# Uneven stores for two octets, work on the last loads moved behind older work, and the last Q evacuation on two engines, in a one-core linear ReLU attention kernel

## The chip, the cores and the metric

One core of a Trainium2 chip. The metric is the device time of one execution in microseconds (us). The span in a profile runs from the first to the last instruction of one profiled execution and is some 1.8 us shorter than that time. A core has five compute engines (PE does matmuls, DVE and ACT elementwise work, POOL, but for building the identity matrix, and SP here only issue transfers) and sixteen DMA engines that move all data between HBM and the on-chip memory.

## The reference

```python
batch, heads, seq, dim = 8, 12, 512, 64           # float32
Q_feat, K_feat = np.maximum(0, Q), np.maximum(0, K)
KV    = np.einsum('bhkd,bhkv->bhdv', K_feat, V)    # 64 x 64 per head
K_sum = np.sum(K_feat, axis=2)
numerator   = np.einsum('bhqd,bhdv->bhqv', Q_feat, KV)
denominator = np.einsum('bhqd,bhd->bhq', Q_feat, K_sum)
return numerator / (denominator[:, :, :, None] + 1e-10)
```

Three inputs of 12.58 MB are read and one output of the same size is written: 50.33 MB for very little arithmetic.

## The kernel before

The 96 heads are handled in 12 octets of 8 heads. Each octet has two groups g of K and V (256 KB each on chip, as bf16) and one Q. `prep` makes the masked bf16 operands, `mm_kv` forms K^T V and the sum of K, `transp` and `evac_qt` transpose Q and apply the ReLU, `mm_out` and `norm` (three rounds) give the output, `store` writes 1 MB. Order on each engine is the order of the program. The cut below is shortened, and its comments are added.

```python
def evac_qt(o, i):
    ...
    for z in range(2):
        nc.scalar.activation(qtz[o % NZ][:, z, us, :, z, :], pv[:, :, :, z, :], Act.Relu)

def store(o, o_sb):
    if o + DELAY < NO:       # a dummy copy: holds the store until K of octet o+5 has landed
        nc.sync.dma_start(out=scratch, in_=k_sb[2 * (o + DELAY)][0:1, 0, :])
    parts = 2 if o == NO - 1 else 1
    ...                      # whole store of 128 rows of 8 KB; the last octet's in two halves
# ...
for o in range(NO + 1):      # octet o is prepared while octet o-1 is put out
    if o < NO:  mm_kv(2 * o); evac_kv(2 * o)
    if o > 0:   mm_out(o - 1, 0); norm(o - 1, 0, o_sb)
    if ahead:   prep(2 * o + 2); prep_act(2 * o + 2)
    if o > 0:   mm_out(o - 1, 1); norm(o - 1, 1, o_sb)
    if o < NO:  mm_kv(2 * o + 1); evac_kv(2 * o + 1); ...   # and Q of octet o
    if ahead:   prep(2 * o + 3); prep_act(2 * o + 3)
    if o > 0:   mm_out(o - 1, 2); norm(o - 1, 2, o_sb); store(o - 1, o_sb)
```

All loads but the first four are issued from POOL and cast from float32 to bf16 on the way (one software queue); all stores are issued from SP (one hardware queue). Both queues run on the same sixteen DMA engines (point 2 of the prediction; here the two account for 73.9% and 27.1% of the sixteen engines' time).

## Time and profile before

| | before |
|---|---|
| time, median of 6 runs | 128.02 us (127.97 to 128.18) |
| profiled span | 126.2 us |
| HBM traffic | 50.33 MB, 399 GB/s over the span |
| last two half stores issued | 119.02 us and 1 us later |
| last mark of the last store | 125.28 us |

A *mark* is the moment at which one DMA engine reports that its share of one transfer has landed; a transfer over sixteen engines leaves sixteen marks in the trace. They are read here from the trace's record of semaphore updates, sorted by time; the record does not say which engine a mark comes from. The page and the stages of this kernel are shown in the prediction. One more view carries the argument, the waits of SP's queue (waiting line, what it waited for: us in total, times, longest):

```profile
SPq L197 <- DMA k_sb<-in_K_dram: 71.9, 7, 41.3
SPq L197 <- DMA scratch<-k_sb: 22.8, 6, 4.3
SPq L202 <- DVE o_sb L187: 9.0, 4, 5.9
```

SP's time goes into waiting for K, on purpose: stores are held back so that loads run first, and a backlog of finished octets is left for the end. Little of its waiting is for results (9.0 us in this row).

### The profile page before, as it was taken

How to read it: one execution, taken by the hardware profiler on the slowest of the kernel's cores; microseconds unless marked ns; L12 is line 12 of the kernel's file. 1: busy time of each engine (PE TensorE's matmuls, PEld its weight loads, DVE VectorE, ACT ScalarE, POOL GpSimd, SP SyncE). 2: the span in 40 equal slices, each digit the busy share in tenths (PEclk: the TensorE clock that was granted, in tenths of full speed). 3: DMA queues.
4: the chain of work that ended last, by engine and by line, in shares of the span. 5: the costliest groups of instructions: out<-in, count | busy, mean ns of one | idle time of the engine just before them, and what ended most of it. 6: DMA issues, size and time to landing. Idle time of an engine off the chain costs nothing.

```text
span 126.2 us, 4865 instructions
## 1 busy us (share of the span) xinstructions
PE 77.3 (61%) x2112; PEld 68.3 (54%) x2112; DVE 80.6 (64%) x210; ACT 76.9 (61%) x169; POOL 32.1 (25%) x62
## 2 busy tenths in 40 slices
PE   0032917978397956534997647389964793797200
PEld 0041907967386845434986646178953692696100
DVE  3256785698936959673669787528828628774900
ACT  0165891599198798660799949508917925958000
POOL 6902424325243331241143133033113000000000
PEclk9999999999859999996799999955999679769995
DMA  3999999999999999999999999999999999999992
GB/s 106 374 309 213 214 208 209 217 206 218 205 215 209 208 214 324 257 216 325 256 215 301 280 214 281 301 212 214 347 235 216 316 266 216 352 418 410 416 384 104
DMA packets 10757, 32.81 MB, mean 260 GB/s; under 512 B 1392, under 2 KB 1392, under 8 KB 9328
## 3 DMA queue, kind: packets, MB, share of 16 engines
q0 software_dynamic: 8064, 17.83, 73.9%
q1 hardware_dynamic: 2384, 13.63, 27.1%
q10 hardware_dynamic: 288, 1.05, 2.1%
q8 instruction: 16, 0.26, 0.7%
q14 instruction: 5, 0.04, 0.1%
HBM read 37.75 MB, written 12.58 MB: 399 GB/s over the span
## 4 chain that ended last, share of the span: by engine, by line
DMA 32%; PE 27%; issue 13%; ACT 11%; DVE 10%; ACTq 1%; SPq 0%
DMA v_sb<-in_V_dram 25%; PE ps_out L174 13%; PE ps_kv L139 11%; DMA kv_first<-in_K_dram 7%; ACT kvd L146 5%; ACT qt L159 4%; PE ps_qt L153 3%; DVE o_sb L187 3%; DVE qt L121 3%; ACT vo L134 3%; DVE kf L128 2%; DVE vo L130 1%; DVE rec L186 1%; ACTq L267 0%; DVE kvd L118 0%
## 5 line engine op out<-in xcount | busy, mean ns | idle before, releaser
L139 PE MATMUL ps_kv<-vo,kf 128*128 128x130 bf16 x384 | 32.5, 248 | 21.9 <-ACT vo L134 11.7
L174 PE MATMUL ps_out<-kvd,qt 128*32 128x130 bf16 x1536 | 33.7, 243 | 16.7 <-issue 13.3
L139 PEld LDWEIGHTS <-kf 128*128 128x128 bf16 x384 | 27.8, 112 | 25.3 <-DVE vo L130 16.3
L174 PEld LDWEIGHTS <-qt 128*32 128x32 bf16 x1536 | 27.0, 107 | 21.9 <-issue 15.3
L146 ACT CAST kvd<-ps_kv 64x130 bf16<-64x130 f32 x96 | 25.2, 263 | 16.7 <-PE ps_kv L139 14.8
L134 ACT ACTIVATE vo<-v_sb,mask 128x1024 bf16<-128x1024 bf16 x22 | 26.2, 1190 | 13.9 <-DMA v_sb<-in_V_dram 13.8
L187 DVE TENSOR_TENSOR o_sb<-ps_out,rec 128x768 f32<-128x768 f32 (+1 forms) x36 | 31.3, 868 | 1.4
L159 ACT ACTIVATE qt<-ps_qt 128x512 bf16<-128x512 bf16 x48 | 24.8, 603 | 0.3
L128 DVE TENSOR_SCALAR kf<-k_sb,mask 128x1024 bf16<-128x1024 bf16 x44 | 19.1, 476 | 8.6 <-DMA k_sb<-in_K_dram 8.6
L85 POOL DMA_DIRECT2D k_sb<-in_K_dram x22 | 12.8, 583 | 39.1 <-DMA q_sb<-in_Q_dram 24.1
L184 DVE TENSOR_SCALAR den<-ps_out 128x12 f32<-128x12 f32 (+1 forms) x36 | 5.9, 164 | 17.9 <-PE ps_out L174 17.8
L153 PE MATMUL ps_qt<-ident,q_sb 128*128 128x128 bf16 x192 | 15.7, 245 | 2.4 <-issue 2.4
L87 POOL DMA_DIRECT2D v_sb<-in_V_dram x22 | 12.3, 557 | 17.1 <-DMA k_sb<-in_K_dram 7.3
L153 PEld LDWEIGHTS <-q_sb 128*128 128x128 bf16 x192 | 14.0, 112 | 2.6 <-issue 2.5
L130 DVE TENSOR_SCALAR vo<-v_sb,mask 128x1024 bf16<-128x1024 bf16 x22 | 10.6, 481 | 2.1 <-DMA v_sb<-in_V_dram 2.1
L186 DVE RECIPROCAL rec<-den 128x12 f32<-128x12 f32 (+1 forms) x36 | 7.9, 220 | 1.2
L91 POOL DMA_DIRECT2D q_sb<-in_Q_dram x12 | 6.5, 542 | 7.8 <-DMA v_sb<-in_V_dram 4.1
L128 DVE TENSOR_SCALAR kf<-kv_first,mask 128x1024 bf16<-128x1024 f32 x4 | 2.8, 750 | 4.9 <-DMA kv_first<-in_K_dram 4.9
L134 ACT ACT_TABLE_LOAD x1 | 1.3, 1283 | 5.8 <-DMA kv_first<-in_V_dram 5.8
L121 DVE MEMSET qt<- 128x2048 f32 x2 | 3.5, 1765 | 0.8 <-issue 0.8
L134 ACT ACTIVATE vo<-kv_first,mask 128x1024 bf16<-128x1024 f32 x2 | 2.4, 1180 | 2.6 <-DMA kv_first<-in_V_dram 2.6
L130 DVE TENSOR_SCALAR vo<-kv_first,mask 128x1024 bf16<-128x1024 f32 x2 | 1.5, 747 | 0.0
(12 smaller groups left out, 3.5 us busy)
## 6 DMA issues: line engine op xcount, KB each, us to landing
out_dram<-o_sb SPq DMA_DIRECT2D x11, 1024.0 KB, 9.2
q_sb<-in_Q_dram POOLq DMA_DIRECT2D x12, 512.0 KB, 14.9
k_sb<-in_K_dram POOLq DMA_DIRECT2D x22, 256.0 KB, 13.8
v_sb<-in_V_dram POOLq DMA_DIRECT2D x22, 256.0 KB, 13.2
kv_first<-in_V_dram ACTq DMA_DIRECT2D x2, 512.0 KB, 7.3
kv_first<-in_K_dram SPq DMA_DIRECT2D x2, 512.0 KB, 7.0
out_dram<-o_sb SPq DMA_DIRECT2D x2, 512.0 KB, 5.1
scratch<-k_sb SPq DMA_DIRECT2D x7, 0.1 KB, 5.1
```

The costliest lines, as they stand in the source:

```text
L85: nc.gpsimd.dma_start(out=k_sb[g].rearrange("p r d -> p (r d)"), in_=Kr[g])
L87: nc.gpsimd.dma_start(out=v_sb[g].rearrange("p r d -> p (r d)"), in_=Vr[g])
L128: nc.vector.tensor_scalar(kf[g][:, :, s, :], k_sb[g], scalar1=0.0, scalar2=mask[:, 0, s:s + 1], op0=Alu.max, op1=Alu.mult)
L130: nc.vector.tensor_scalar(vo[g % NB][:, :, 0, 0:D], v_sb[g], scalar1=mask[:, 1, 0:1], scalar2=None, op0=Alu.mult)
L134: nc.scalar.activation(vo[g % NB][:, :, 1, 0:D], v_sb[g], Act.Copy, scale=mask[:, 1, 1:2])
L139: nc.tensor.matmul(ps_kv[g], kf[g][:, r, :, :].rearrange("p s d -> p (s d)"), vo[g % NB][:, r, :, :], start=(r == 0), stop=(r == R - 1), s ...
L146: nc.scalar.copy(kvd[g % NK][64 * c:64 * c + 64, :, s, c, :], ps_kv[g][64 * s:64 * s + 64])
L153: nc.tensor.transpose(ps_qt[o, i][:, u, :], q_sb[o][:, i * (U // 2) + u, :], ident)
L159: nc.scalar.activation(qtz[o % NZ][:, z, us, :, z, :], pv[:, :, :, z, :], Act.Relu)
L174: nc.tensor.matmul(po[hs, b, c:c + 2 * D1], qtf[o % NZ][:, z, u * P + 32 * w:u * P + 32 * w + 32], kvd[(2 * o + h // 4) % NK][:, h % 4 // ...
L186: nc.vector.reciprocal(rec, den)
L187: nc.vector.tensor_tensor(o_sb[:, 2 * u0:2 * (u0 + nu)].rearrange("p (b r) d -> p b r d", b=2), pv[:, :, :, 0:D], rec.unsqueeze(3).to_broa ...
```

## The change

Intent: give engines that have less to do more rows of a store; keep the in-order engines from standing at loads that come late in the last two octets; halve the last evacuation of Q by using two engines.

```diff
-    def evac_qt(o, i):
+    def evac_qt(o, i, eng=None):
...
         for z in range(2):
-            nc.scalar.activation(...)
+            if eng is nc.vector:
+                eng.tensor_scalar(qtz[o % NZ][:, z, us, :, z, :], pv[:, :, :, z, :], scalar1=0.0,
+                                  scalar2=None, op0=Alu.max)
+            else:
+                nc.scalar.activation(...)
...
+    def cuts(o):
+        return ((16, P), (0, 5), (5, 10), (10, 15), (15, 16)) if o in (1, 3) else ((0, P),)
...
+        for p0, p1 in cuts(o):
+            nc.sync.dma_start(out=Ov[p0:p1], in_=o_sb[p0:p1])
...
     for o in range(NO + 1):
...
+        if o < NO - 1:
+            kv(2 * o)
+        if o > 0:
+            out_round(o - 1, 0, o_sb)
+        if o < NO - 2:
+            prepare(2 * o + 2)
+        if o > 0:
+            out_round(o - 1, 1, o_sb)
+        if o < NO - 1:
+            kv(2 * o + 1)
+            qt(o)
+        if o < NO - 2:
+            prepare(2 * o + 3)
+        if o > 0:
+            out_round(o - 1, 2, o_sb)
             store(o - 1, o_sb)
+        if o == NO - 2:
+            prepare(2 * NO - 2)
+        if o == NO - 1:
+            prepare(2 * NO - 1)
+            kv(2 * NO - 2)
+            kv(2 * NO - 1)
+            qt(o)
```

Here `kv` is `mm_kv` with its evacuation, `qt` both transposes with theirs (the second on DVE in the last octet), `prepare` is `prep` with `prep_act`, `out_round` is `mm_out` with `norm`.

More of the change, by code (lines that the diff above doesn't have):

```diff
@@ L158, in evac_qt @@
         for z in range(2):
-            nc.scalar.activation(qtz[o % NZ][:, z, us, :, z, :], pv[:, :, :, z, :], Act.Relu)
+            if eng is nc.vector:
+                eng.tensor_scalar(qtz[o % NZ][:, z, us, :, z, :], pv[:, :, :, z, :], scalar1=0.0,
+                                  scalar2=None, op0=Alu.max)
+            else:
+                nc.scalar.activation(qtz[o % NZ][:, z, us, :, z, :], pv[:, :, :, z, :], Act.Relu)
     ROUNDS = ((0, 6), (6, 6), (12, 4))
@@ L197, in store @@
             nc.sync.dma_start(out=scratch, in_=k_sb[2 * (o + DELAY)][0:1, 0, :])
-        parts = 2 if o == NO - 1 else 1
-        n = RQ // parts
-        for j in range(parts):
-            rs = slice(n * j, n * (j + 1))
-            nc.sync.dma_start(out=Or[o].rearrange("p (r d) -> p r d", d=D)[:, rs], in_=o_sb[:, rs])
+        Ov = Or[o].rearrange("p (r d) -> p r d", d=D)
+        if o == NO - 1:
+            for j in range(2):
+                rs = slice(RQ // 2 * j, RQ // 2 * (j + 1))
+                nc.sync.dma_start(out=Ov[:, rs], in_=o_sb[:, rs])
+            return
+        for p0, p1 in cuts(o):
+            nc.sync.dma_start(out=Ov[p0:p1], in_=o_sb[p0:p1])
     zero(0)
@@ L213, with kv, qt, prepare @@
     zero_q(1)
+    def kv(g):
+        mm_kv(g)
+        evac_kv(g)
+    def qt(o):
+        for i in range(2):
+            transp(o, i)
+            evac_qt(o, i, nc.vector if o == NO - 1 and i == 1 else None)
+    def prepare(g):
+        prep(g)
+        prep_act(g)
+    def out_round(o, j, o_sb):
+        mm_out(o, j)
+        norm(o, j, o_sb)
     for o in range(NO + 1):
-        ahead = o + 1 < NO
         if o > 0:
             o_sb = outp.tile([P, RQ, D], fp32, name="o_sb", tag="o_sb")
-        if o < NO:
-            mm_kv(2 * o)
-            evac_kv(2 * o)
+        if o < NO - 1:
+            kv(2 * o)
         if o > 0:
-            mm_out(o - 1, 0)
-            norm(o - 1, 0, o_sb)
-        if ahead:
-            prep(2 * o + 2)
-            prep_act(2 * o + 2)
-        if o > 0:
-            mm_out(o - 1, 1)
-            norm(o - 1, 1, o_sb)
-        if o < NO:
-            mm_kv(2 * o + 1)
-            evac_kv(2 * o + 1)
-            for i in range(2):
-                transp(o, i)
-                evac_qt(o, i)
-        if ahead:
-            prep(2 * o + 3)
-            prep_act(2 * o + 3)
+            out_round(o - 1, 0, o_sb)
+        if o < NO - 2:
+            prepare(2 * o + 2)
+        if o > 0:
+            out_round(o - 1, 1, o_sb)
[4 more added lines that the diff above has]
+            prepare(2 * o + 3)
         if o > 0:
-            mm_out(o - 1, 2)
-            norm(o - 1, 2, o_sb)
+            out_round(o - 1, 2, o_sb)
             store(o - 1, o_sb)
+        if o == NO - 2:
+            prepare(2 * NO - 2)
+        if o == NO - 1:
+            prepare(2 * NO - 1)
+            kv(2 * NO - 2)
+            kv(2 * NO - 1)
+            qt(o)
 _INS = ['Q', 'K', 'V']
```

## The prediction

> **What bounds the kernel now.** I read four things in this order: the page's slices over time and its DMA table, the stages at the end, the timeline of the last 22 us, and the completion marks that the trace keeps for each DMA. First the page (section 2, 3 and 6):
>
> ```profile
> DMA  3999999999999999999999999999999999999992
> GB/s 106 374 309 213 214 208 209 217 206 218 205 215 209 208 214 324 257 216 325 256 215 301 280 214 281 301 212 214 347 235 216 316 266 216 352 418 410 416 384 104
> ...
> q0 software_dynamic: 8064, 17.83, 73.9%
> q1 hardware_dynamic: 2384, 13.63, 27.1%
> ...
> q8 instruction: 16, 0.26, 0.7%
> ...
> HBM read 37.75 MB, written 12.58 MB: 399 GB/s over the span
> ...
> out_dram<-o_sb SPq DMA_DIRECT2D x11, 1024.0 KB, 9.2
> ...
> out_dram<-o_sb SPq DMA_DIRECT2D x2, 512.0 KB, 5.1
> ```
>
> The DMA row is 9 in every slice but the first and the last, while no compute engine is above 64% of the span. The GB/s row looks lower during the loads only because loads cast float32 to bf16 and the row counts what was written; in bytes of HBM it is 50.33 MB at 399 GB/s throughout. So the kernel is bound by its sixteen DMA engines from start to end. What matters is when the slowest of the sixteen runs dry. Now the stages at the end (columns: stretch, length, busy time of PE, PEld, DVE, ACT, POOL, clock, DMA share, GB/s):
>
> ```profile
> 110.00:115.00 5.00, 4.58 (x120) 4.06 (x112) 3.05 (x9) 3.61 (x11) 0.00 (x0) 0.75 1.01 413
> 115.00:120.00 5.00, 2.33 (x128) 1.83 (x124) 4.18 (x10) 1.27 (x3) 0.00 (x0) 1.00 1.00 417
> 120.00:126.20 6.20, 0.00 (x0) 0.00 (x0) 0.02 (x1) 0.00 (x0) 0.00 (x0) 0.72 0.58 240
> ```
>
> From 110 us on there are only stores, at 413 to 417 GB/s. After 120.0 us there is no compute, yet 240 GB/s times 6.2 us = 1.49 MB are still moved, against 1.05 MB in the last octet's store: when the last compute ended, 0.44 MB of the store before it was still queued. The last result did not make the slowest engine wait. The timeline of the late part:
>
> ```profile
> 104.08 0.88 DVE L128 TENSOR_SCALAR kf<-k_sb,mask 128x1024 bf16<-128x1024 bf16 x2 [2.35 <-DMA k_sb<-in_K_dram]
> ...
> 105.38 1.18 ACT L134 ACTIVATE vo<-v_sb,mask 128x1024 bf16<-128x1024 bf16 x1 [3.54 <-DMA v_sb<-in_V_dram]
> ...
> 107.73 2.06 ACT L159 ACTIVATE qt<-ps_qt 128x512 bf16<-128x512 bf16 x4
> ...
> 112.80 1.05 PE L153 MATMUL ps_qt<-ident,q_sb 128*128 128x128 bf16 x16
> ...
> 114.21 2.06 ACT L159 ACTIVATE qt<-ps_qt 128x512 bf16<-128x512 bf16 x4
> ...
> 119.33 0.69 DVE L187 TENSOR_TENSOR o_sb<-ps_out,rec 128x512 f32<-128x512 f32 x1
> ```
>
> DVE and ACT stand 2.35 and 3.54 us at late loads although older work (the evacuation of octet 10's Q, done only at 107.73) is ready behind them: this is what the second part of the change attacks. Last, the completion marks. The last half store's sixteen engines report, in us: 122.76, 122.79, 122.81, 122.83, 122.94, then 123.41, 123.53, 123.97, then 124.56, 124.93, 124.95, 124.97, 124.99, 125.08, 125.10, 125.28. So five engines are done 2.4 us before the last, three are in between, eight are late. The spread grows from 0.6 us at 20 us, and grows by one engine and some 0.9 us with each of the 16 instruction fetches (16 KB, mean 0.94 us each, from 25.0 to 118.6 us): seven of sixteen marks are late by that at 62 to 64 us, and around 82 us the load's marks stand as eight on time, six late, two doubly late. Eight engines carry two fetches each.
>
> **What the Trainium skill says.** (1) "DMA: Bandwidth & Descriptors", section on why a DMA increments its semaphore by 16: the number k of engines is the largest up to 16 that divides the slowest dimension, and on the hardware queue it is the lowest-numbered k. So 112 partitions go to 16 engines, 7 each; 5 partitions to engines 0 to 4, one each. Nothing in this trace shows a store with k under 16, so this is taken on trust. (2) Same page, section "Issuing engines are not separate DMA queues": all queues share the sixteen engines; the trace agrees (no gain left once the DMA row is 9). (3) "Runtime: NRT & Kernel Launch", section "Instruction fetch mechanics": instructions are refilled in blocks of 16 KiB; the trace agrees (16 packets of 16384 bytes, 0.26 MB). (4) "VectorE: DVE Perf Modes", section "Why PSUM operands drop a tier": a PSUM source limits the mode, so I do not count on a fast DVE evacuation.
>
> **The change part by part.** First, stores of octets 1 and 3. Before: 8 rows of 8 KB on each engine. After: 7 on each, and three more on each of engines 0 to 4; the single partition is one row, on engine 0 if it goes to one engine (or 512 bytes on each). Per octet engines 5 to 15 lose one row, engines 1 to 4 gain two, engine 0 two or three. A row of 8192 bytes takes 309 ns in the trace and the next starts 3 ns before its end, so 0.306 us. Two octets: -0.61 us on eleven engines, +1.22 us on four, +1.22 to +1.84 us on engine 0. If the five early engines are engines 0 to 4: they end at 122.8 + 1.22 = 124.0, engine 0 at 124.0 to 124.7; the late ones at 125.28 - 0.61 = 124.67. The end moves by -0.61 us. That these five are the lowest-numbered is my inference: I chose it because exactly five stand apart, as the stores of 5 rows want[...]. Extra issues: eight more on SP at about 0.53 us (the median of its store issues), while SP mostly waits for K loads (71.9 us in its own waits): hidden.
>
> Second, the order of the last two octets. What moves: preparing K/V groups 22 and 23 goes behind the output rounds of octets 9 and 10, and both their matmuls and octet 11's transposes go behind octet 10's outputs. By the durations of the timeline, octet 10's Q is evacuated at 104.3 to 106.3 instead of 107.7 to 109.8; group 22 is prepared on DVE at 105.7 to 107.1; three rounds of normalising (1.4, 1.4, 1.1 us) run to 111.0, so store 10 is ready near 111 instead of 115.6. But group 23's preparation (1.37 us) now lies behind them, to 112.4; its matmuls end at 113.6, transposes at 114.5; ACT copies KV to 114.9 and evacuates its half of Q by 115.95.
>
> Third, the Q halves: four ACT instructions of 0.515 us become two there and two on DVE. A DVE instruction of 128x512 out of PSUM took 0.69 us, so DVE's pair takes up to 1.4 us, beside ACT's 1.03: about 0.7 us saved on this chain, already in the times above. The last output rounds then start at 116.0 instead of 114.86, but without octet 10's normalising among them, and the last normalising ends at about 120.7 by this hand schedule, against 120.0 before: between 1 us earlier and 1 us later, near zero. What is it worth? In the trace before, the first half of the last store was issued at 119.02 and its first packets on the early engines came some 1.2 us later; there they were waited for by 0.3 us, on early engines only. After the change these finish store 10 at 121.1 and the others at up to 122.2, so an issue up to 119.9 for the first half and up to about 121.2 for the second costs nothing. Second and third part: 0 us. Sum: -0.6 us, 127.98 - 0.61 = 127.4 us.
>
> **The rivals.** (a) Compute sets the end, so the reordering pays: then the time falls by what the last normalising moves, 1 us or so, to 126.8. For it: the critical chain on the page ends in compute. Against it: 0.44 MB still queued at 120.0 and late engines that run store 10, and both halves of 11, without a gap. (b) The five early engines are not numbers 0 to 4, or only some are. Then a late engine gains 1.2 to 1.8 us: 129.2 to 129.8. Against it: the five-fold split itself, which would have no reason. (c) The lengthened compute tail becomes the wait: with the last normalising at 122 instead of 120.7 the store of 0.5 MB would follow late, +0.5 us or so, giving 127.9 in all. (d) Loads get later because engines 0 to 4 lag 0.6 to 0.9 us after store 1 (near 52 us) and 1.2 to 1.8 us after store 3 (near 62 us), when few fetches have delayed the others: waits in the middle grow, but the engines stay busy, so the end does not move.
>
> **Range and chances.** The sixteen last marks average 124.2, so perfect balance gives at most 1.1 us; a gain over 2% (2.6 us) is out of what this change can reach. The three runs before lie within 0.16 us. I take 127.4, with 126.8 (balance plus some compute gain) and 128.1 (compute tail eats the gain) as limits; beyond lies rival (b), at about one in ten. Faster by over 2%: 0.02, slower by over 2%: 0.02, within: 0.96.
>
> **What would show it.** Right: the last store's marks within about 1 us instead of 2.5, the last at 124.7; the small stores on five engines; last DVE normalising between 119 and 121 with the DMA share still near 1.0 before 120; octet 10's Q evacuation on ACT before the late V preparation. Wrong: marks that spread further, with one to five of them past 126 (rival b); a gap in the store traffic before the last halves (rival c); an end that moves by more than 1.1 us, which balance cannot give.

## The result, and the profile after

The changed kernel took 127.53 us (median of 6 runs, 127.32 to 127.67) against 128.02 us of the kernel before in the same rounds: ratio 0.9957, 95% interval 0.9944 to 0.9970. Ratios here and below are the mean time of one kernel's runs over that of the other's of the same rounds, so not quite the ratio of the medians quoted. Executions over 1.5% slower than the fastest of the same kernel are left out of the means. The gain is 0.49 us by the medians; 0.61 was forecast, and 127.53 lies in the stated range of 126.8 to 128.1.

The page of the changed kernel answers with these lines (busy tenths of the DMA engines in 40 slices, and the HBM traffic):

```profile
DMA  3999999999999999999999999999999999999993
...
HBM read 37.75 MB, written 12.58 MB: 401 GB/s over the span
```

Nothing in the regime has changed: the DMA row is full between the first and the last slice, the bytes are the same, and the rate has gone from 399 to 401 GB/s, which is the gain. The stages at the end (columns as in the prediction):

```profile
110.00:115.00 5.00, 3.29 (x48) 2.84 (x52) 1.96 (x6) 2.70 (x9) 0.00 (x0) 0.73 1.00 415
115.00:120.00 5.00, 2.35 (x124) 1.99 (x112) 3.59 (x9) 0.00 (x0) 0.00 (x0) 0.93 0.98 406
120.00:125.60 5.60, 0.00 (x0) 0.00 (x0) 0.00 (x0) 0.00 (x0) 0.00 (x0) 0.73 0.64 265
```

In the last stretch 265 GB/s times 5.6 us are again 1.48 MB for a last store of 1.05 MB: at 120 us the queues still held a part of the store before it. The timeline of the changed kernel (start, length, what) shows the new order:

```profile
103.70 2.06 ACT L163 ACTIVATE qt<-ps_qt 128x512 bf16<-128x512 bf16 x4
...
105.03 0.87 DVE L128 TENSOR_SCALAR kf<-k_sb,mask 128x1024 bf16<-128x1024 bf16 x2
...
105.63 1.20 ACT L134 ACTIVATE vo<-v_sb,mask 128x1024 bf16<-128x1024 bf16 x1
...
109.32 0.69 DVE L191 TENSOR_TENSOR o_sb<-ps_out,rec 128x512 f32<-128x512 f32 x1
...
113.61 1.08 ACT L163 ACTIVATE qt<-ps_qt 128x512 bf16<-128x512 bf16 x2
114.11 0.76 DVE L160 TENSOR_SCALAR qt<-ps_qt 128x512 bf16<-128x512 bf16 x2 [2.91 <-PE ps_qt L153]
...
118.85 1.37 SPq L211 DMA_DIRECT2D out_dram<-o_sb  x2
...
119.17 0.69 DVE L191 TENSOR_TENSOR o_sb<-ps_out,rec 128x512 f32<-128x512 f32 x1
```

Octet 10's Q is evacuated at 103.70 instead of 107.73, the preparation of the late group no longer stands at its load (no wait is printed at 105.03 and 105.63, where there were 2.35 and 3.54 us), and octet 10 is finished at 110.0 instead of 115.6. Yet the last normalising ends at 119.86, only 0.16 us before that of the kernel before: what was won in octet 10 was given back, as group 23 and octet 11's Q now come behind it. The sixteen marks of the last half store, before and after:

```
before  122.76 122.79 122.81 122.83 122.94 | 123.41 123.53 123.97 | 124.56 124.93 124.95 124.97 124.99 125.08 125.10 125.28
after   122.64 122.66 122.78 | 123.82 124.01 124.10 124.14 124.15 124.25 124.27 124.31 124.39 124.56 124.57 124.62 124.69
```

The mean hardly moves (124.06 and 124.00): the work is the same. (Readings of "last minus mean" need this check: when engines wait for the last store, the mean moves too.) What moves is the last one, from 125.28 to 124.69, by 0.59 us; from "last 1.22 us behind the mean" to "0.69 us behind it". The small stores show their engines too: each store of 5 partitions leaves five marks (61.28 to 61.64 us for the first one), the store of one partition leaves one (63.03 us). The span ends 0.90 or 0.91 us after the last mark of the last half store in both profiles, and in those of every kernel below without probes, save 1.16 us with 112 + 8 + 8.

### The profile page after: what moved, and what is told of

It is laid out like the page before. It is cut to its first block, busy times and chain, and to the rows that moved or that the text cites. A ratio compares the mean times of both kernels' runs of the same rounds, so it can differ in the third digit from the quotient of the medians.

```text
span 125.6 us, 4876 instructions
## 1 busy us (share of the span) xinstructions
PE 78.7 (63%) x2112; PEld 69.4 (55%) x2112; DVE 81.2 (65%) x212; ACT 76.0 (61%) x167; POOL 31.7 (25%) x62
## 3 DMA queue, kind: packets, MB, share of 16 engines
q10 hardware_dynamic: 288, 1.05, 2.1%
## 4 chain that ended last, share of the span: by engine, by line
DMA 32%; PE 30%; DVE 15%; issue 12%; ACT 6%; SPq 0%; ACTq 0%
DMA v_sb<-in_V_dram 25%; PE ps_out L178 14%; PE ps_kv L139 12%; DMA kv_first<-in_K_dram 7%; DVE o_sb L191 5%; PE ps_qt L153 4%; DVE kf L128 3%; DVE qt L121 3%; ACT qt L163 3%; ACT kvd L146 2%; DVE vo L130 2%; DVE rec L190 1%; ACT vo L134 1%; DVE den L188 1%; DVE kvd L118 0%
## 5 line engine op out<-in xcount | busy, mean ns | idle before, releaser
L139 PE MATMUL ps_kv<-vo,kf 128*128 128x130 bf16 x384 | 33.6, 253 | 22.2 <-ACT vo L134 10.1
L139 PEld LDWEIGHTS <-kf 128*128 128x128 bf16 x384 | 28.6, 114 | 25.6 <-DVE vo L130 16.9
L163 ACT ACTIVATE qt<-ps_qt 128x512 bf16<-128x512 bf16 x46 | 23.8, 603 | 0.3
L153 PE MATMUL ps_qt<-ident,q_sb 128*128 128x128 bf16 x192 | 16.3, 251 | 1.2 <-issue 0.9
L153 PEld LDWEIGHTS <-q_sb 128*128 128x128 bf16 x192 | 14.6, 116 | 1.4 <-issue 1.0
L160 DVE TENSOR_SCALAR qt<-ps_qt 128x512 bf16<-128x512 bf16 x2 | 0.8, 420 | 2.9 <-PE ps_qt L153 2.9
```

The source lines that it names most:

```text
L139: nc.tensor.matmul(ps_kv[g], kf[g][:, r, :, :].rearrange("p s d -> p (s d)"), vo[g % NB][:, r, :, :], start=(r == 0), stop=(r == R - 1), s ...
L153: nc.tensor.transpose(ps_qt[o, i][:, u, :], q_sb[o][:, i * (U // 2) + u, :], ident)
```

## The experiments

Twelve kernels were run in three sets, each set on one chip with its own runs of the kernel before. "Last - mean" is the last mark of the last half store minus the mean of its sixteen marks, in the profiled run.

| kernel | median us | before in the same set | ratio (95%) | last - mean, us |
|---|---|---|---|---|
| the change, with the prediction | 127.53 | 128.02 | 0.9957 (0.9944 to 0.9970) | 0.69 |
| the change again | 127.46 | 127.98 | 0.9962 (0.9948 to 0.9976) | 0.66 |
| split alone | 127.90 | 128.10 | 0.9983 (0.9970 to 0.9996) | 1.16 |
| split alone, again | 127.72 | 127.98 | 0.9982 (0.9970 to 0.9994) | 1.02 |
| order and DVE half alone | 128.02 | 128.10 | 0.9991 (0.9979 to 1.0003) | 1.26 |
| change without the DVE half | 127.56 | 128.00 | 0.9970 (0.9957 to 0.9984) | 0.72 |
| change, last store delayed | 127.76 | 128.00 | 0.9982 (0.9968 to 0.9996) | 0.63 |
| split on four octets | 129.06 | 128.10 | 1.0073 (1.0061 to 1.0086) | 1.31 |
| 112 + 8 + 8 | 128.51 | 127.98 | 1.0035 (1.0022 to 1.0049) | 1.50 |
| mix of both splits | 128.00 | 127.98 | 1.0000 (0.9986 to 1.0015) | 1.27 |
| before, half of PE's code | 126.89 | 128.10 | 0.9905 (0.9892 to 0.9918) | 0.87 |

The two kernels with probes were run once each and are not in the table.

### The split alone

The kernel before with the changed kernel's `cuts` and `store`, and nothing else of the change.

> Only the split of the two stores, in the kernel before. Theory (the sixteen DMA engines set the end, and only the split shifts their work): the whole gain, -0.5 to -0.6 us, so 127.4 to 127.5; three engines' last marks stay near 122.7 and thirteen lie at 124.0 to 124.7. Rival (compute sets the end and the new order brings the gain): 128.0.

Measured: 127.90 us, a ratio of 0.9983: 0.2 us, clear of zero but less than half of what both the forecast and this expectation said. The marks are as expected for fifteen engines (three at 122.35 to 122.47, twelve at 123.83 to 124.71), and a single one is at 125.20. (The expectation had thirteen from 124.0 to 124.7.) Its last store was not issued late; SP's timeline of this kernel says

```profile
118.53 1.62 SPq L208 DMA_DIRECT2D out_dram<-o_sb  x2
```

which is 0.3 us earlier than with the whole change. So the compute's end is not what the split alone lacks.

### The order alone

```diff
-        return (...) if o in (1, 3) else ((0, P),)
+        return (...) if o in () else ((0, P),)
```

> The changed kernel with whole stores for octets 1 and 3: the new order and the Q half on DVE alone. Theory: 128.0 as before (within 0.15 us), although store 10 is ready some 5 us earlier; the last mark stays at about 125.3. Rival: 127.5, the gain of the change.

Measured: 128.02 us, ratio 0.9991 with an interval that contains 1; last mark 125.45. Alone, the new order with the DVE half is worth nothing that can be told from zero.

### The dose doubled

```diff
-        ... if o in (1, 3) else ((0, P),)
+        ... if o in (1, 2, 3, 4) else ((0, P),)
```

> The split on octets 1, 2, 3 and 4 instead of 1 and 3: the dose doubled. Theory with engines 0 to 4 as the five early ones: engine 0 takes twelve rows of 0.306 us more and ends at 122.9 + 3.7 = 126.6, four others at 125.3, the rest at 124.1 or earlier; 129.2 to 129.4 in all, over a us slower than before. If the early five were other engines, a late one takes the rows: 130.4 to 131.9. Rival (any split of the stores helps): another -0.5, 126.9.

Measured: 129.06 us, last mark 126.49 where 126.6 was computed for engine 0. Only the last mark fits that closely: four others were computed at 125.3, and the four marks before the last lie at 125.58 to 126.20. Splitting is not good in itself: it moves rows of 0.306 us from some engines to others, and at twice the dose, by the computed ends, the receivers end last. The split pays only as far as it evens out. Two other things show here. Loads suffered as rival (d) of the prediction said (the store that is held until octet 11's K has landed was issued at 106.06 us, with the change at 104.18), and SP's timeline has the last store at

```profile
120.70 1.77 SPq L211 DMA_DIRECT2D out_dram<-o_sb  x2
```

1.85 us later than with the change; and nine marks lie between 124.62 and 124.76, which reads as nine engines that were waiting for it. Here, unlike in the changed kernel, most engines were waiting for the compute.

### Why eight engines are late

The prediction ascribed the late engines to instruction fetches, from counting. The kernel before was run with half of PE's instructions removed (1056 matmuls and 1056 weight loads instead of 2112 of each), wrong results, the same transfers:

```diff
-        for r in range(R):
+        for r in range(R // 4):
...
-            for z in range(2):
+            for z in range(1):
```

> The kernel before with half of the tensor engine's instructions left out (one of two heads in the output matmuls, 4 of 16 K/V matmuls; the result is wrong on purpose), the same DMAs. Theory (the eight late engines are late by two instruction fetches each): 8 fetches of 16 KB instead of 16, the late eight late by one fetch, 0.94 us: the last mark near 124.4, 127.1 in all, and the eight late ones no more than 1.2 us behind the early ones. Rival (those engines are late for another reason, such as slower ports): last mark 125.3 and 128.0, spread 2.5 us as before.

Measured: 126.89 us. The page's line for the instruction queue (packets, MB, share of the engines):

```profile
q8 instruction: 8, 0.13, 0.4%
```

Eight fetches instead of sixteen, the last mark at 124.13 instead of 125.28, the spread 1.93 instead of 2.52 us. The rival (slow ports) would have left both. But the spread was expected at 1.2 us or less, and the marks no longer part into two groups: the fetches are not all of the spread, and what the rest is stays open. The drop is larger than forecast by 0.2 us: in the trace before, a fetch holds its engine for 0.935 us and the data packet behind it takes 0.705 instead of 0.309 us (fetch at 113.09 us), so this fetch cost its engine 1.33 us. By this estimate eight fewer are 8 x 1.33 / 16 = 0.67 us of the mean; the mean mark fell by 0.80. One reservation: PE's work was halved as well, and the last store was issued 2.0 us earlier, at 117.00. The experiments on delay below say how little that is worth.

### The change and the split again, side by side

The split alone and the change had been measured in different sets, so both were run again in one, unchanged.

> The changed kernel once more, on the same chip and beside the same runs of before as the split alone, since split alone (-0.2 us) and order alone (-0.1 us) were measured apart from it and do not add up to -0.55. Theory A (the parts are worth what their sum says and the rest is the scatter of one engine): 127.7 to 127.8, less than 0.15 us from the split alone. Theory B (the new order is worth something only once the stores are balanced): 127.5, with the split alone 0.3 us behind it.

> The split alone once more. Theory A: within 0.15 us of the changed kernel of the same rounds. Theory B: 127.8 to 127.9, some 0.3 us behind it, with one engine's last mark 0.4 to 0.5 us behind the next as in its first profile.

Measured: 127.46 us for the change (0.9962), 127.72 us for the split alone (0.9982). Both repeat their first ratio. The split alone stays 0.26 us behind, and five of the six runs of the change lie below its fastest. By this, theory B: beside the split the new order is worth some 0.26 us, although alone it showed 0.1 us, not told from zero. The intervals don't exclude that its worth is the same in both cases (0.15 to 0.2 us).

The two profiles do not show where the 0.26 us come from. That of the change is of its slowest run (127.79 us), that of the split of its fastest (127.71), and the last marks lie within 0.02 us of each other:

```
split alone, again  122.52 122.53 122.62 123.75 123.87 124.03 124.06 124.08 124.08 124.42 124.44 124.53 124.70 124.78 124.81 125.04
the change again    123.25 123.30 123.39 123.75 124.09 124.39 124.45 124.55 124.65 124.66 124.74 124.82 124.84 124.86 124.95 125.02
```

The change's last mark is nearer to its mean (0.66 against 1.02 us) only because the mean is later, 124.36 against 124.02: its last store was issued at 119.50 instead of 118.65, and the early marks came later. In the split the last mark stands 0.23 us behind the next, where theory B had 0.4 to 0.5.

### Two other ways to balance

```diff
# 112 + 8 + 8
-        return ((16, P), (0, 5), (5, 10), (10, 15), (15, 16)) if o in (1, 3) ...
+        return ((16, P), (0, 8), (8, 16)) if o in (1, 3) ...
# mix: the line above for octets 1 and 3, and for octet 2 the split of the change
```

> Octets 1 and 3 as 112, 8 and 8 partitions, otherwise the changed kernel. Theory: engines 0 to 7 gain one row each per octet, 8 to 15 lose one: late eight at 124.67 as with the change, early five at 123.5 instead of 124.0 to 124.6, middle three at about 123.9 instead of 122.7. The same time as the changed kernel, within 0.15 us, if the late eight set its end; if engine 0 with its third row sets it, 0.1 us faster or more.

> A balance made from the marks: stores of octets 1 and 3 as 112, 8 and 8 partitions, of octet 2 as 112, 5, 5, 5 and 1. Theory (rows per engine decide): the late eight lose three rows, 125.28 - 0.92 = 124.4; the early five gain four (engine 0 five), 124.1 to 124.4; the middle three gain one or two, about 123.7; last mark 124.4 against 124.7 of the changed kernel: 0.3 us faster than it, 127.2. If the middle three are not engines 5 to 7, a late engine gains rows: last mark 125.6 or more, 128.4. Rival (compute now sets the end): no faster than the changed kernel.

Both expectations failed: 128.51 us, slower than before by 0.5 us, and 128.00 us, no gain at all (for a wrong map of the engines the second expectation had said 128.4). With 112 + 8 + 8, eight marks lie at 124.08 to 124.40 (late engines relieved of two rows, as computed) but three at 124.77, 125.05 and 125.56. That reads as engines that were late already and got more rows: the guess that engines 5 to 7 are the middle three, and not the rule of rows per engine, would be at fault. The next runs looked at it.

### Which engines are early

Five tiny loads of 5, 8, 12, 1 and 3 partitions were queued behind the last store. By the rule in point (1) of the prediction each runs on the lowest-numbered engines, and its marks tell when those had drained. A mark names no engine: the numbers here and below rest on that rule, and what the runs show is how many marks there are and when they come.

```diff
+    for k in (5, 8, 12, 1, 3):
+        pr = consts.tile([P, 16], fp32, name=f"probe{k}")
+        nc.sync.dma_start(out=pr[0:k], in_=Kr[0][0:k, 0:16])
```

> The kernel before with five tiny loads of 5, 8, 12, 1 and 3 partitions queued behind the last store: they run on the lowest 5, 8, 12, 1, 3 engines, and each mark tells when that engine's queue had drained. If engines 0 to 4 are the early five and 5 to 7 the middle three: the five marks of the first all lie before 124 us, the eight of the second before 124.5, and four of the twelve of the third at 125 or later. If some of engines 5 to 7 are late: marks of 125 or later among the eight. Span some 0.5 us longer.

> The same behind the changed kernel. Theory (the split puts 4 rows of 0.306 us on engines 0 to 4, 6 on engine 0): the five marks at 124.0 to 124.8 with engine 0 as the last of them, and three of the eight marks, engines 5 to 7, the earliest of all at about 123.

The marks of the first two probes of each (single runs of 128.49 and 128.27 us, state unknown, used only for the order of marks):

```
behind before, 5 partitions:  123.97 124.00 124.01 124.06 124.17
behind before, 8 partitions:  124.05 124.14 124.18 124.19 124.24 124.36 124.59 125.18
behind after,  5 partitions:  124.15 124.59 124.61 124.67 124.90
behind after,  8 partitions:  122.95 123.95 124.33 124.62 124.77 124.79 124.85 125.08
```

In the kernel before, engines 0 to 4 had all drained by 124.17, with late engines' last store marks at 124.83 to 125.48 in that run. So engines 0 to 4 are early: the inference on which the prediction's main step stood holds, as far as one run can show it. (Here the last store was issued at 120.05 us, 1.03 us later than in the first profile, and its eight earliest marks lie together at 123.80 to 123.99. The run shows the five among these eight, not apart from the three.) But one mark of the eight is at 125.18, so one of engines 5 to 7 is late, and giving all eight a row, as in 112 + 8 + 8, loads it further. That accounts for one of the three late marks there. Behind the changed kernel the five have moved to 124.15 to 124.90, among the last, and an engine of 5 to 7 is the first at 122.95. That engine 0, with its third row, is the last of the five could not be told from the marks.

### The last store later

```diff
     def out_round(o, j, o_sb):
         mm_out(o, j)
+        if o == NO - 1 and j == 1:
+            zero_q(0)            # clears a tile that is no longer needed: 1.76 us on DVE
         norm(o, j, o_sb)
```

> The changed kernel with 1.77 us of idle memory clearing on the vector engine between the output rounds of the last octet, so that its last store is issued 1.8 us later. Theory (backlog in the DMA queues hides the end of the compute): first half issued at 120.6, its packets from 121.8, behind store 10 which the late engines end at 122.2; 127.5 to 127.7. Rival (the compute sets the end, which would explain what the new order brought beside the split): 129.2.

Measured: 127.76 us. One of its five runs took 129.6 us and is left out of the ratio. SP's timeline:

```profile
120.28 1.37 SPq L211 DMA_DIRECT2D out_dram<-o_sb  x2
```

The last store was issued 1.43 and 0.78 us later than in the two profiles of the change, and the time rose by 0.23 to 0.30 us over the change's two medians, which are of other sets. Three engines had ended store 10 by 119.63 and waited until about 121.5 for the last store; the latest engine, which ended store 10 at 122.62, had no need to. So the compute's end is nearly covered by the backlog, not fully: about a sixth of the 1.76 us put in came through.

### Without the DVE half

```diff
-            evac_qt(o, i, nc.vector if o == NO - 1 and i == 1 else None)
+            evac_qt(o, i)
```

> The changed kernel with the last Q half back on the scalar engine. The last output rounds start up to 0.7 us later. If the DMA queues hide the end of the compute: 127.5 as the changed kernel, so that what was gained beside the split comes from the order alone. If it counts: 127.7 to 128.2, near the split alone (127.7 to 127.9).

Measured: 127.56 us, ratio 0.9970. Within the scatter that is the changed kernel; the third part of the change moved nothing that can be seen. Its last store was issued at 118.30, so even the hoped-for earlier end did not come from it.

## Why the prediction was right or wrong

**The bound.** Right. The DMA row stayed full, the mean of the marks stayed (124.06 to 124.00), and the time followed the last mark: 0.59 us in the profiles, 0.49 us by the medians. The prediction put the mean of the marks before at 124.2 and so the most that balance can give at 1.1 us; its own sixteen marks average 124.06, which makes it 1.2. And its sign of being right, marks within about 1 us, did not come: they spread over 2.05 us. It contradicts the prediction's own sums, which take 0.61 us from the three middle engines and so leave them at 122.8 to 123.4; the measured first three ended at 122.64 to 122.78.

**Who is early, and why.** Right in what the forecast needed: one probe run puts engines 0 to 4 among the early ones, and halving PE's code halved the fetches and brought the last mark forward by 1.15 us. Fetches are not all of the spread, as 1.93 us of it stayed. Not right, and it cost two experiments their expectation: the later reading that engines 5 to 7 are the three in the middle.

**The split, -0.61 us.** The direction and the rows-per-engine mechanism were right (the doubled dose made the kernel 1 us slower, for 1.1 to 1.3 computed), the size was not: alone it brought 0.20 to 0.26 us. This term of the sum was over-sized. Fifteen of sixteen engines ended by 124.71 and 124.81 us in the two profiles, for a computed 124.7; the time is set by the sixteenth, whose mark stood 0.5 and 0.2 us behind the next one. Which engine that is stays open.

**The order and the DVE half, 0 us.** This is the step that failed, and in the other direction: on top of the split they brought 0.26 us. Rival (a), that the compute's end counts, is not the reason that the runs support: the split alone had its last store issued at 118.53 and 118.65, the change at 118.85 and 119.50, so the faster kernel ended its compute later; and 1.76 us of added work before the last results cost only 0.2 to 0.3 us. Why the order gains stays open. The last mark is earlier in the change's first profile and without the DVE half (124.69 and 124.77) than with the split alone (125.20 and 125.04), but not in the change's second profile (125.02). The fetches fall at other times in the new order (the fifteenth at 109.66 and 110.74 instead of 112.85 and 112.86 us), which may be a part of it. They also differ between profiles of one kernel: their durations come in a pattern of eight, which starts with 935, 974, 975, 962 ns in the change's first profile and with 974, 961, 893, 893 ns, some places on, in its second, so the order of the engines that they hold may differ from run to run. No run separates these. The total of -0.49 us was thus near the forecast of -0.61 by luck in part: an over-sized term and a missed one partly cancelled.

**Sizes in the hand schedule.** Octet 10 was ready at 110.0 (111 forecast); DVE's pair of Q instructions took 0.76 us (up to 1.4 allowed, from a float32 row of the same width, while this source is bf16); the last normalising ended at 119.86 (120.7). None of it reached the time. The split stores ran near 61 and 82 us, not near 52 and 62.

**Rivals.** (b), the early engines being others, would have given 129 us: excluded by the time and by the probe. (c), the tail as a new wait: in the change it did not set the end, but it appears when the tail is pushed, as in the delayed and in the four-octet kernel. (d), loads that lag: not seen to cost at two octets, plain at four, where the last store was issued 1.85 us later.

## What to carry to other kernels

Where all DMA engines are busy from start to end, look at the sixteen completion marks of the last transfer: the time is set by the last of them, and the most that moving rows between engines can gain is the last minus the mean. Look at the mean too, as it moves when engines wait, and compare the profiled run's own time with the median, since one profile is one run. Verify which engines are early with tiny transfers of k partitions before moving rows, since a wrong map makes the kernel slower. Time won inside the compute is worth little while a backlog of finished stores covers it, and parts of a change that were expected to add up should be measured together and apart.

## What the Trainium skill lacked or had wrong

- "Runtime: NRT & Kernel Launch", section "Instruction fetch mechanics", calls the cost of a 16 KiB refill mostly hidden. In a kernel bound by DMA it is not: a refill took 0.935 us of one DMA engine, and the data packet behind it 0.705 instead of 0.309 us. Cutting sixteen refills to eight, with half of PE's code, took 1.2 us (0.95%) off the time.
- No page says on which DMA engines the refills run. The marks name no engine, but their count points to eight engines with two refills each, in turn: after seven refills seven of sixteen marks were late (62 to 64 us), after ten, six were late and two doubly late (82 us), and at the end eight were late. By the probe, engines 0 to 4 were among the early ones.
- "DMA: Bandwidth & Descriptors", section "Latency and other measured facts", says that engines 7 and 15 are usually slower. Until the first refill (25.0 us) no engine stood out: the marks of a load at 20 us lay within 0.65 us. Whether 7 and 15 were among the late ones afterwards, the marks don't tell.
- The same page, section on why a DMA increments its semaphore by 16, is borne out for 5 partitions by the count of marks (five); which engines, the marks don't tell. For a store of one partition with 2048 contiguous elements, which its rule leaves unclear (the slowest dimension that is not 1 has 2048 elements), the runs show a single engine: one mark, at 63.03 and at 83.50 us.
